# Temporary tiles, gate scaling and quad order around the seven-product stage of a hybrid attention and state-space block

## The chip, the cores and the metric

The kernel runs on one core of one Trainium2 chip. The metric is the device time of one execution in microseconds (us), lower is better. A profile is one execution taken by the hardware profiler; its times are given from the start of its span.

## The reference, cut to what matters

One layer of a hybrid block on 256 tokens of width 2048, all in float32:

```python
hn = rms_norm(x, norm_w)
q, k, v, z_a, z_s, xbc, dt_raw, g_a, g_s = split(hn @ w_in)
o_a = dilated_window_attention(q, k, v, three patterns, mixed) * silu(z_a)
y = ssd_chunked_scan(silu(conv(xbc)), softplus(dt_raw + dt_bias), -exp(a_log)) + d_skip * xs
y = rms_norm(y * silu(z_s), ssm_norm_w)                       # 4096 wide
merged = sigmoid(g_a) * (o_a @ w_attn_branch) + sigmoid(g_s) * (y @ w_ssm_branch)
out = rms_norm(x + merged @ w_out, final_norm_w)
```

The change touches three of these products: `y @ w_ssm_branch` (called ssm in the kernel), and the columns of `hn @ w_in` that give `g_a` (called ga) and `v` (called v).

## The kernel before, in words

Every float32 operand of a matmul is split into a high part h and a low part l, each in a reduced float32 format, and a product is three matmuls: high with high, high with low, low with high. Weights are split on the chip: ScalarE (ACT) copies the loaded weights into h, VectorE (DVE) subtracts h from the weights to give l. Weights arrive by DMA through a ring of tiles named w or wq; h and l have rings of their own (hq and lq for the weights of this stage). From line 702 on each ring has six tiles of 1024 columns (four of the pool stream, two of the pool more).

The stages follow one another on TensorE (PE): first the projections for the state-space part with its scan, then ssm, ga and v, then q, k and the gate of the attention head by head with the attention itself, then the two last products.

The stage of the change works in quads. A quad is a block of 256 rows of the right matrix by 1024 columns, four sub-blocks named 11, 12, 21 and 22, stored by columns as 12, 11 (first half) and 22, 21 (second half). The left factor, 256 tokens wide, is cut into two halves of 128 tokens. A plain quad takes eight block products, 24 matmuls. A seven-product quad (`seven`, after Winograd's form of Strassen's scheme) takes seven, 21 matmuls. It needs sums of sub-blocks on both sides:

- on the right side `quad` (line 623) makes two tiles t13 and t24 of 1024 columns from the loaded weights, with four DVE additions (L647), and splits them as well; both tiles have the tag T with two buffers, in the pool that is passed in;
- on the left side `left` (line 594) makes the sums s1 to s4 of the tokens' blocks, for two quads in one pass of its loop: an addition (L601) that gives the tile x, four more operations (L605 to L608) that give the tile raw, and splits of raw by ACT (L610) and DVE (L611) into sf_y or sf_x and, for s4 of ssm, into yT itself. In the profile x and raw are both called tmp. They come from the same tag T with its two buffers as t13 and t24.

`quads` (line 654) runs one half (cc, 1024 columns) of a product: it goes through the quads in a given order, and behind the last seven-product quad (`u == last`) it adds the accumulators that several results share, into four blocks called sums: ACT copies accumulator 1 (L692), DVE adds (L693 to L696). At the end `finish` combines each sum with an accumulator. For ssm, sums is a tile of the pool mid of its own (tag sums, 2048 columns), and `finish` is `gated`: L731 adds, L732 multiplies into the gate tile th_s. For ga and v the sums lie in the result itself (th_a).

For ssm the order of cc 0 is 0, 2, 4, 1, 6, 8, 3, 10, 12, 5, 11, 9, 13, 7, 14, 15, with seven products in the quads 1, 3, 5, 7 and 9; the left factors for these are made by `left` in three passes (quads 1 and 3, quads 5 and 7, quad 9). After the second quad `then` is called, which is `norm_y` (line 706): eight small matmuls give the sums of squares of y, DVE and GpSimd make the factor (L339, L341, L343, written into the tile small), and two ACT instructions (L716) scale the gate tile th_s, 2048 columns each, with the factor as scale and bias.

After ssm its pool mid is closed and a pool mid2 is opened for ga and v, with T alone in it. `left` is called there for four quads of XT; only the factors of the quads 1, 3 and 5 are used.

The order of the instructions on each engine is set before the run by a planner (`schedule_with_timeline_sim=True`, line 916): it goes by program order as priority, and the splits of the weights in `unit` and `quad` stand 120 places ahead (`L_AHEAD`). Each engine then runs its own list in that order. Within a quad stage the splits of the weights, and the L647 additions, keep their order among themselves (`in_turn`).

Of the kernel before, what the change touches and what calls it, by code (L numbers as in the profile page):

```python
# [9 lines left out]
F32 = mybir.dt.float32  # L10
F32R = mybir.dt.float32r
# [4 lines left out]
P = 128  # L16
# [146 lines left out]
def hybrid_block(ctx: ExitStack, tc: tile.TileContext, wall, wq, xt, x, pk_d, cst_d, fw_d, out):  # L163
# [427 lines left out]
        gates(("gs", 3), th_s, XT)  # L591
        tick(final=True)

    def left(tmp, src, n, h3, l3, h4, l4):
        v = src.rearrange("p (n r) c -> p n r c", r=4)[:, :, 2:4, :]
        for a in range(0, n, 2):
            m = min(2, n - a)
            js = slice(a, a + m)
            x = tmp().rearrange("p (n k s) -> p n k s", n=2, k=2)[:, :m]
            raw = tmp().rearrange("p (n e s) -> p n e s", n=2, e=4)[:, :m]  # L600
            ve.tensor_tensor(x, v[:, js, :, :S].bitcast(F32), v[:, js, :, S:].bitcast(F32), ALU.add)  # L601
            a11, a21 = x[:, :, 0, :P], x[:, :, 0, P:]
            a12, a22 = x[:, :, 1, :P], x[:, :, 1, P:]
            s1, s2, s3, s4 = (raw[:, :, j] for j in range(4))
            ve.tensor_tensor(s1, a22, a21, ALU.subtract)  # L605
            ve.scalar_tensor_tensor(s2, s1, -1.0, a11, ALU.mult, ALU.subtract)
            ve.tensor_tensor(s3, a11, a21, ALU.subtract)
            ve.tensor_tensor(s4, a12, s2, ALU.add)  # L608
            for r, h, l in ((raw[:, :, :3], h3[:, js], l3[:, js]), (s4, h4[:, js], l4[:, js])):
                ac.activation(h, r, AF.Copy)  # L610
                ve.tensor_tensor(l, r, h.bitcast(F32), ALU.subtract)  # L611
# [8 lines left out]
            )  # L620
        behind[key] = ins.ins.name

    def quad(pool, n, seven):
        ws = []
        for j in range(2):
            ws.append(ring("w", f"wq{n}_{j}"))
            nc.sync.dma_start(ws[j], wq[n, :, j * UNIT : (j + 1) * UNIT])
        parts = {}

        def halves(src, names, cut=0):  # L630
            h, l = ring("h", f"hq{n}_{names[1]}"), ring("l", f"lq{n}_{names[1]}")
            in_turn("h", ac.activation(h[:, cut:], src[:, cut:], AF.Copy))  # L632
            in_turn("l", ve.tensor_tensor(l[:, cut:], src[:, cut:], h[:, cut:].bitcast(F32), ALU.subtract))  # L633
            for j, name in enumerate(names):
                parts[name] = h[:, j * 512 : j * 512 + 512], l[:, j * 512 : j * 512 + 512]

        with tc.high_priority(L_AHEAD):
            halves(ws[0], ("12", "11"), 512 if seven else 0)
            halves(ws[1], ("22", "21"))
            if seven:  # L640
                b12, b11, b22, b21 = (w[:, c : c + 512] for w in ws for c in (0, 512))
                t13, t24 = (pool.tile([P, UNIT], F32, name=f"t{n}_{e}", tag="T", bufs=2) for e in range(2))
                for t, a, b in (
                    (t13[:, :512], b12, b11), (t13[:, 512:], b12, b22),
                    (t24[:, :512], t13[:, :512], b22), (t24[:, 512:], t24[:, :512], b21),
                ):
                    in_turn("l", ve.tensor_tensor(t, a, b, ALU.add))  # L647
                halves(t13, (5, 7))
                halves(t24, (6, 4))
        return parts  # L650

    BANKS = {1: "g", 2: "g", 6: "g", 3: "g", 7: "m1", 4: "m1", 5: "m2", 8: "m2"}

    def quads(pool, tag, cc, x_of, n_kt, order, lefts, sums, finish, then=None):
        accs = {}
        last = [u for u in order if u in lefts][-1]

        def product(b, x, w, stop=False):
            first = b not in accs
            if first:  # L660
                accs[b] = bank(BANKS[b], 4 if BANKS[b] == "g" else 2, f"ps_{tag}{cc}_{b}")
            pe.matmul(accs[b], x[0], w[0], start=first, stop=False)  # L662
            pe.matmul(accs[b], x[0], w[1], start=False, stop=False)  # L663
            pe.matmul(accs[b], x[1], w[0], start=False, stop=stop)  # L664

        def block(kt, i):
            x = x_of(kt)
            return x[:, i * P : (i + 1) * P], x[:, S + i * P : S + (i + 1) * P]

        for n, u in enumerate(order):  # L670
            w = quad(pool, QFIRST[tag, cc] + u, u in lefts)
            end = n == len(order) - 1
            k0, k1 = 2 * u, 2 * u + 1
            if u in lefts:
                s1, s2, s3, s4 = lefts[u]
                z = u == last
                product(1, block(k0, 0), w["11"], z)
                product(2, block(k1, 0), w["21"], end)
                product(3, s4, w["22"], end)
                product(7, s3, w[7], z)  # L680
                product(5, s1, w[5], z)
                product(6, s2, w[6], z)
                product(4, block(k1, 1), w[4], end)
            else:
                for b, i, c in ((2, 0, "1"), (3, 0, "2"), (4, 1, "1"), (8, 1, "2")):
                    product(b, block(k0, i), w["1" + c])
                    product(b, block(k1, i), w["2" + c], end)
            if then and n == 1:
                then()
            if u == last:  # L690
                (p1, u4), (u3, u5) = sums
                ac.activation(p1, accs[1], AF.Copy)  # L692
                ve.tensor_tensor(u4, accs[6], p1, ALU.add)  # L693
                ve.tensor_tensor(u3, accs[7], u4, ALU.add)
                ve.tensor_tensor(u4, accs[5], u4, ALU.add)
                ve.tensor_tensor(u5, accs[5], u3, ALU.add)  # L696
        for i, c, b, op in (
            (0, 0, 2, ALU.add), (0, 1, 3, ALU.subtract), (1, 0, 4, ALU.add), (1, 1, 8, ALU.subtract),
        ):
            finish(i, 2 * cc + c, accs[b], sums[i][c], op)  # L700

    more = ctx.enter_context(tc.tile_pool(name="more", bufs=2))
    for tag, dt in (("w", F32), ("h", F32R), ("l", F32R)):
        more.tile([P, UNIT], dt, name=f"first_{tag}", tag=tag, bufs=MORE)
    with tc.tile_pool(name="mid", bufs=2) as mid:
        def norm_y():
            tot = bank("m2", 2, "tot_y")
            for i in range(2):
                for n in range(2):
                    pe.matmul(  # L710
                        tot[:, 2 * i : 2 * i + 2], ssq[:, n, i * P : (i + 1) * P], ones2,
                        start=(n == 0), stop=(n == 1),
                    )
            _, hr = rsqrt_rows(tot[:, 0:4:2], INNER, "y")
            for i in range(2):
                ac.activation(th_s[:, i], th_s[:, i], AF.Identity, scale=hr[:, i : i + 1], bias=hr[:, i : i + 1])  # L716

        sf = mid.tile([P, 5, 2, 3, P], F32R, name="sf_y", tag="sf", bufs=1)
        lefts = {}
        for m, n in enumerate((4, 1)):  # L720
# [1 line left out]
            h3, l3 = s6[:, :, 0], s6[:, :, 1]  # L722
            v = yT[m].rearrange("p (n r) c -> p n r c", r=4)[:, :n, 2]
            h4, l4 = v[:, :, P:S], v[:, :, S + P :]
            left(lambda: mid.tile([P, 1024], F32, name="tmp", tag="T", bufs=2), yT[m], n, h3, l3, h4, l4)
            for j in range(n):
                lefts[8 * m + 2 * j + 1] = [(h3[:, j, e], l3[:, j, e]) for e in range(3)] + [(h4[:, j], l4[:, j])]

# [2 lines left out]
            ve.tensor_tensor(b, a, b, op)  # L731
            ve.tensor_tensor(g, g, b, ALU.mult)  # L732

        for cc, order in enumerate(
            ((0, 2, 4, 1, 6, 8, 3, 10, 12, 5, 11, 9, 13, 7, 14, 15), (1, 0, 2, 3, 4, 6, 5, 8, 10, 7, 11, 12, 9, 13, 14, 15))
        ):
            sums = mid.tile([P, 2, 2, 512], F32, name=f"sums{cc}", tag="sums", bufs=1)
            sums = [[sums[:, i, c] for c in range(2)] for i in range(2)]
            quads(
                mid, "ssm", cc, lambda kt: yT[kt // 16][:, kt % 16, :], 2 * KT, order, lefts, sums, gated,  # L740
                norm_y if cc == 0 else None,
            )

    yo1 = big.tile([P, 2, 2, D], F32, name="th_a", tag="yo1")
    th_a, vt = yo1[:, 0], yo1[:, 1]
    with tc.tile_pool(name="mid2", bufs=2) as mid:
        sf = big.tile([P, 4, 2, 4, P], F32R, name="sf_x", tag="yo0")
        h4, l4 = sf[:, :, 0], sf[:, :, 1]
        left(
            lambda: mid.tile([P, 1024], F32, name="tmp", tag="T", bufs=2), XT, 4,  # L750
            h4[:, :, :3], l4[:, :, :3], h4[:, :, 3], l4[:, :, 3],
        )
        lefts = {2 * j + 1: [(h4[:, j, e], l4[:, j, e]) for e in range(4)] for j in range(4)}

        def gate(i, c, a, b, op):
            ve.tensor_tensor(b, a, b, op)
# [5 lines left out]
        for tag, dst, finish in (("ga", th_a, gate), ("v", vt, value)):  # L762
            for cc in range(2):
                order = (0, 1, 2, 3, 4, 5, 6, 7) if cc or tag == "v" else (0, 2, 4, 1, 6, 3, 5, 7)
                some = {u: lefts[u] for u in (1, 3, 5)}
                sums = [[dst[:, i, (2 * cc + c) * 512 : (2 * cc + c + 1) * 512] for c in range(2)] for i in range(2)]
                quads(mid, tag, cc, lambda kt: XT[:, kt, :], KT, order, some, sums, finish)

    with tc.tile_pool(name="att", bufs=2) as ap, tc.tile_pool(name="ev2", bufs=2) as ev, tc.tile_pool(name="odd2", bufs=2) as odd:
        masks = ap.tile([P, 768], F32, name="masks", tag="masks", bufs=1)  # L770
# [149 lines left out]
```

## Time and profile before

| | |
|---|---|
| median of 3 runs | 1414.25 us (1414.15 to 1415.11) |
| the profiled execution, its own time | 1415.89 us |
| its span, first to last instruction | 1414.1 us |
| mean granted TensorE clock | 0.995 |
| PE busy | 1393.3 us (99%) |
| DVE busy | 1053.8 us (75%) |
| ACT busy | 791.7 us (56%) |
| ssm on PE | 587.61 to 766.43 us |
| ga on PE | 766.43 to 851.36 us |
| v on PE | 851.36 to 934.32 us |

How to read the profile: busy time counts instructions that are in work, for PE with modelled ends; PEld is the loading of weights into TensorE. PEclk is the clock that TensorE was granted, 1.00 or 9 tenths and more at full speed. In a timeline a row gives start, duration, engine, line, operation, output and inputs; `x3` means that three instructions that follow one another are merged, and square brackets give the idle time before the row and what ended it.

### The profile page before, as it was taken

Reading aid. Unit: us, or ns where it says so; the run is one execution under the profiler, and the core shown is the slowest. Engines: PE = TensorE matmul, PEld = TensorE weight load, DVE = VectorE, ACT = ScalarE, POOL = GpSimd, SP = SyncE. Lnnn points to the kernel's source line nnn. Section 1 sums busy time; section 2 is a strip of 40 time slices with the busy share of each in tenths; the row PEclk is TensorE's granted clock in tenths of the full one; section 3 lists DMA queues with packets and bytes.
Section 4 is the critical chain, followed back from the end, with each engine's and each line's share of the span. In section 5 each row is a group of like instructions: output and inputs, shape, how many; then the busy total and the mean of one; then the engine's idle time right before and its main releaser. Section 6 shows DMA issues by size and latency. Waiting matters only on the chain.

```text
span 1414.1 us, 19876 instructions
## 1 busy us (share of the span) xinstructions
PE 1393.3 (99%) x7338; PEld 1183.8 (84%) x7338; DVE 1053.8 (75%) x1551; ACT 791.7 (56%) x1222; POOL 10.1 (1%) x64
## 2 busy tenths in 40 slices
PE   9999999999999999989999999999999999999997
PEld 7788888888888888868888788888888888888886
DVE  5978888877788888778978998876666666655653
ACT  6657766747575757455444566445544545444441
POOL 0000000000000000000000000000000000000000
PEclk9999999999999999989999999999999999999999
DMA  8567656566656666556665575675555555576652
GB/s 330 181 197 229 202 177 210 169 208 203 186 170 211 196 190 183 166 162 205 211 212 190 181 229 182 210 238 179 174 170 176 169 175 171 173 268 186 187 179 74
DMA packets 78049, 272.39 MB, mean 193 GB/s; under 512 B 8768, under 2 KB 9344, under 8 KB 77312
## 3 DMA queue, kind: packets, MB, share of 16 engines
q1 hardware_dynamic: 77376, 270.08, 61.1%
q8 instruction: 57, 0.93, 0.3%
q10 hardware_dynamic: 576, 1.05, 0.2%
q14 instruction: 40, 0.33, 0.1%
HBM read 268.93 MB, written 2.16 MB: 192 GB/s over the span
## 4 chain that ended last, share of the span: by engine, by line
PE 94%; DVE 3%; ACT 1%; issue 1%; DMA 1%; SPq 0%; POOL 0%; POOLq 0%; DVEq 0%; ACTq 0%
PE ps_xs L261 8%; PE ps_zs L261 8%; PE ps_xs L264 4%; PE ps_q L261 4%; PE ps_k L261 4%; PE ps_za L261 4%; PE ps_zs L264 4%; PE ps_ssm L662 4%; PE ps_ssm L663 4%; PE ps_ssm L664 4%; PE ps_k L264 2%; PE ps_za L264 2%; PE ps_q L264 2%; PE ps_attn L329 2%; PE ps_attn L328 2%; PE ps_attn L327 2%
## 5 line engine op out<-in xcount | busy, mean ns | idle before, releaser
L224 DVE TENSOR_TENSOR l<-w,h 128x1024 fp32r<-128x1024 f32 (+1 forms) x353 | 426.6, 1212 | 235.4 <-ACT h L223 232.9
L223 ACT ACTIVATE h<-w 128x1024 fp32r<-128x1024 f32 (+1 forms) x353 | 368.9, 1049 | 373.8 <-PE ps_za L261 50.7
L261 PE MATMUL ps_xs<-XT,h 128*128 128x512 f32 x496 | 174.9, 394 | 0.0
L261 PE MATMUL ps_zs<-XT,h 128*128 128x512 f32 x496 | 174.4, 394 | 0.0
L633 DVE TENSOR_TENSOR lq<-wq,hq 128x1024 fp32r<-128x1024 f32 (+1 forms) x128 | 138.2, 1129 | 39.1 <-ACT hq L632 39.1
L632 ACT ACTIVATE hq<-wq 128x1024 fp32r<-128x1024 f32 (+1 forms) x128 | 119.1, 979 | 67.4 <-PE ps_ssm L664 27.1
L264 PE MATMUL ps_xs<-XT,l 128*128 128x256 f32 x496 | 139.4, 281 | 0.0
L264 PE MATMUL ps_zs<-XT,l 128*128 128x256 f32 x496 | 138.8, 280 | 0.0
L261 PEld LDWEIGHTS ps_zs<-XT,h 128*128 128x128 f32 x496 | 92.9, 187 | 21.4
L261 PEld LDWEIGHTS ps_xs<-XT,h 128*128 128x128 f32 x496 | 93.0, 187 | 21.1
L264 PEld LDWEIGHTS ps_xs<-XT,l 128*128 128x128 f32 x496 | 93.6, 189 | 0.1
L264 PEld LDWEIGHTS ps_zs<-XT,l 128*128 128x128 f32 x496 | 93.6, 189 | 0.0
L261 PE MATMUL ps_q<-XT,h 128*128 128x512 f32 x256 | 90.4, 392 | 0.0
L261 PE MATMUL ps_za<-XT,h 128*128 128x512 f32 x256 | 89.7, 392 | 0.0
L261 PE MATMUL ps_k<-XT,h 128*128 128x512 f32 x256 | 89.7, 392 | 0.0
L632 ACT ACTIVATE hq<-t 128x1024 fp32r<-128x1024 f32 x44 | 46.1, 1060 | 74.0 <-DVE t L647 47.7
L663 PE MATMUL ps_ssm<-lq,yT 128*128 128x512 f32 x216 | 84.3, 390 | 0.0
L664 PE MATMUL ps_ssm<-hq,yT 128*128 128x512 f32 x216 | 84.1, 390 | 0.0
L662 PE MATMUL ps_ssm<-hq,yT 128*128 128x512 f32 x216 | 79.0, 395 | 0.0
L264 PE MATMUL ps_q<-XT,l 128*128 128x256 f32 x256 | 74.5, 291 | 0.0
L264 PE MATMUL ps_k<-XT,l 128*128 128x256 f32 x256 | 71.7, 280 | 0.0
L264 PE MATMUL ps_za<-XT,l 128*128 128x256 f32 x256 | 71.7, 280 | 0.0
(290 smaller groups left out, 2875.6 us busy)
## 6 DMA issues: line engine op xcount, KB each, us to landing
w<-in_wall SPq DMA_DIRECT2D x352, 512.0 KB, 3.7
wq<-in_wq SPq DMA_DIRECT2D x128, 512.0 KB, 4.6
acb<-acum_d SPq DMA_DIRECT2D x32, 256.0 KB, 3.3
th_s<-in_x SPq DMA_DIRECT2D x1, 2048.0 KB, 10.3
fin<-in_x SPq DMA_DIRECT2D x1, 2048.0 KB, 9.2
early<-in_xt SPq DMA_DIRECT2D x7, 256.0 KB, 7.2
fw<-in_fw SPq DMA_DIRECT2D x1, 1024.0 KB, 11.3
out<-fin SPq DMA_DIRECT2D x4, 256.0 KB, 3.0
```

The lines of the kernel that those rows point to most:

```text
L223: ac.activation(h[:, a:b], w[:, a:b], AF.Copy)
L224: ve.tensor_tensor(l[:, a:b], w[:, a:b], h[:, a:b].bitcast(F32), ALU.subtract)
L261: pe.matmul(acc[:width], h[:, kk, :], m, start=(kt == 0), stop=False)
L264: pe.matmul(acc[:width, S:], l[:, kk, :], m[:, :S], start=False, stop=(kt == n_kt - 1))
L327: pe.matmul(accs[i], xh, h, start=(kt == 0), stop=False)
L328: pe.matmul(accs[i], xh, l, start=False, stop=False)
L329: pe.matmul(accs[i], xl, h, start=False, stop=(kt == n_kt - 1))
L632: in_turn("h", ac.activation(h[:, cut:], src[:, cut:], AF.Copy))
L633: in_turn("l", ve.tensor_tensor(l[:, cut:], src[:, cut:], h[:, cut:].bitcast(F32), ALU.subtract))
L662: pe.matmul(accs[b], x[0], w[0], start=first, stop=False)
L663: pe.matmul(accs[b], x[0], w[1], start=False, stop=False)
L664: pe.matmul(accs[b], x[1], w[0], start=False, stop=stop)
```

## The change

- `left` takes its two temporary tiles from the tags s0 and s1 (one buffer of 1024 columns each) by the new function `two`, no longer from T. The sums of ssm now use the same two tags, and are allocated when the last seven-product quad has been issued (`sums` is now a function that is called at that place).
- `norm_y` no longer scales the gate. `scale_gs` scales a piece of 1024 columns of one token half; four pieces are issued, after the quads at places 9 and 11 of cc 0 and after those at places 2 and 4 of cc 1 (places count from 0).
- The order of ssm cc 0 becomes 0, 2, 4, 6, 1, 8, 3, 10, 5, 12, 7, 11, 9, 13, 14, 15: the first seven-product quad stands at place 4, it was at 3, the last at 12, it was at 13 (quad 9, it was quad 7), and between them every second quad has seven products.
- The pool mid stays open from ssm to v; mid2 is gone.
- `left` is called for three quads of XT, it was four; sf_x has three parts.

```diff
-    def left(tmp, src, n, h3, l3, h4, l4):
-        v = src.rearrange("p (n r) c -> p n r c", r=4)[:, :, 2:4, :]
+    def left(src, n, h3, l3, h4, l4):
+        v = src.rearrange("p (n r) c -> p n r c", r=4)[:, :n, 2:4, :]
...
-            x = tmp().rearrange("p (n k s) -> p n k s", n=2, k=2)[:, :m]
-            raw = tmp().rearrange("p (n e s) -> p n e s", n=2, e=4)[:, :m]
+            x, raw = two("left")
+            x = x.rearrange("p (n k s) -> p n k s", n=2, k=2)[:, :m]
+            raw = raw.rearrange("p (n e s) -> p n e s", n=2, e=4)[:, :m]
...
-                t13, t24 = (pool.tile([P, UNIT], F32, name=f"t{n}_{e}", tag="T", bufs=2) for e in range(2))
+                t13, t24 = (mid.tile([P, UNIT], F32, name=f"t{n}_{e}", tag="T", bufs=2) for e in range(2))
...
-            if then and n == 1:
-                then()
+            if n in then:
+                then[n]()
             if u == last:
+                sums = sums()
...
+        def two(name):
+            return [mid.tile([P, UNIT], F32, name=f"{name}_{e}", tag=f"s{e}", bufs=1) for e in range(2)]
...
-            _, hr = rsqrt_rows(tot[:, 0:4:2], INNER, "y")
-            for i in range(2):
-                ac.activation(th_s[:, i], th_s[:, i], AF.Identity, scale=hr[:, i : i + 1], bias=hr[:, i : i + 1])
+            rsqrt_rows(tot[:, 0:4:2], INNER, "y")
+
+        def scale_gs(cc, i):
+            g, r = th_s[:, i, cc * 1024 : (cc + 1) * 1024], hrs[:, 1, i : i + 1]
+            ac.activation(g, g, AF.Identity, scale=r, bias=r)
...
-        for cc, order in enumerate(
-            ((0, 2, 4, 1, 6, 8, 3, 10, 12, 5, 11, 9, 13, 7, 14, 15), (1, 0, 2, 3, 4, 6, 5, 8, 10, 7, 11, 12, 9, 13, 14, 15))
+        def ssm_sums(cc):
+            return [[t[:, c * 512 : (c + 1) * 512] for c in range(2)] for t in two(f"sums{cc}")]
+
+        for cc, order, then in (
+            (0, (0, 2, 4, 6, 1, 8, 3, 10, 5, 12, 7, 11, 9, 13, 14, 15), {1: norm_y, 9: (0, 0), 11: (0, 1)}),
+            (1, (1, 0, 2, 3, 4, 6, 5, 8, 10, 7, 11, 12, 9, 13, 14, 15), {2: (1, 0), 4: (1, 1)}),
         ):
-            sums = mid.tile([P, 2, 2, 512], F32, name=f"sums{cc}", tag="sums", bufs=1)
-            sums = [[sums[:, i, c] for c in range(2)] for i in range(2)]
...
-    with tc.tile_pool(name="mid2", bufs=2) as mid:
-        sf = big.tile([P, 4, 2, 4, P], F32R, name="sf_x", tag="yo0")
+        sf = big.tile([P, 3, 2, 4, P], F32R, name="sf_x", tag="yo0")
...
+        left(XT, 3, h4[:, :, :3], l4[:, :, :3], h4[:, :, 3], l4[:, :, 3])
+        lefts = {2 * j + 1: [(h4[:, j, e], l4[:, j, e]) for e in range(4)] for j in range(3)}
```

More of the change, by code (lines that the diff above doesn't have):

```diff
@@ L621, in in_turn, with quad @@
         behind[key] = ins.ins.name
-    def quad(pool, n, seven):
+    def quad(n, seven):
         ws = []
@@ L652, in hybrid_block, with quads @@
     BANKS = {1: "g", 2: "g", 6: "g", 3: "g", 7: "m1", 4: "m1", 5: "m2", 8: "m2"}
-    def quads(pool, tag, cc, x_of, n_kt, order, lefts, sums, finish, then=None):
+    def quads(tag, cc, x_of, n_kt, order, lefts, sums, finish, then={}):
         accs = {}
@@ L670, in quads @@
         for n, u in enumerate(order):
-            w = quad(pool, QFIRST[tag, cc] + u, u in lefts)
+            w = quad(QFIRST[tag, cc] + u, u in lefts)
             end = n == len(order) - 1
@@ L724, in hybrid_block @@
             h4, l4 = v[:, :, P:S], v[:, :, S + P :]
-            left(lambda: mid.tile([P, 1024], F32, name="tmp", tag="T", bufs=2), yT[m], n, h3, l3, h4, l4)
+            left(yT[m], n, h3, l3, h4, l4)
             for j in range(n):
@@ L732, in gated @@
             ve.tensor_tensor(g, g, b, ALU.mult)
-        for cc, order in enumerate(
-            ((0, 2, 4, 1, 6, 8, 3, 10, 12, 5, 11, 9, 13, 7, 14, 15), (1, 0, 2, 3, 4, 6, 5, 8, 10, 7, 11, 12, 9, 13, 14, 15))
-        ):
-            sums = mid.tile([P, 2, 2, 512], F32, name=f"sums{cc}", tag="sums", bufs=1)
-            sums = [[sums[:, i, c] for c in range(2)] for i in range(2)]
+        def ssm_sums(cc):
[3 more added lines that the diff above has]
+            (1, (1, 0, 2, 3, 4, 6, 5, 8, 10, 7, 11, 12, 9, 13, 14, 15), {2: (1, 0), 4: (1, 1)}),
+        ):
+            then = {n: f if callable(f) else lambda f=f: scale_gs(*f) for n, f in then.items()}
             quads(
-                mid, "ssm", cc, lambda kt: yT[kt // 16][:, kt % 16, :], 2 * KT, order, lefts, sums, gated,
-                norm_y if cc == 0 else None,
-            )
-    yo1 = big.tile([P, 2, 2, D], F32, name="th_a", tag="yo1")
-    th_a, vt = yo1[:, 0], yo1[:, 1]
-    with tc.tile_pool(name="mid2", bufs=2) as mid:
-        sf = big.tile([P, 4, 2, 4, P], F32R, name="sf_x", tag="yo0")
+                "ssm", cc, lambda kt: yT[kt // 16][:, kt % 16, :], 2 * KT, order, lefts, lambda: ssm_sums(cc), gated, then
+            )
+        yo1 = big.tile([P, 2, 2, D], F32, name="th_a", tag="yo1")
+        th_a, vt = yo1[:, 0], yo1[:, 1]
+        sf = big.tile([P, 3, 2, 4, P], F32R, name="sf_x", tag="yo0")
         h4, l4 = sf[:, :, 0], sf[:, :, 1]
[L749 to L753, printed above, removed]
+        left(XT, 3, h4[:, :, :3], l4[:, :, :3], h4[:, :, 3], l4[:, :, 3])
+        lefts = {2 * j + 1: [(h4[:, j, e], l4[:, j, e]) for e in range(4)] for j in range(3)}
         def gate(i, c, a, b, op):
@@ L764, in hybrid_block @@
                 order = (0, 1, 2, 3, 4, 5, 6, 7) if cc or tag == "v" else (0, 2, 4, 1, 6, 3, 5, 7)
-                some = {u: lefts[u] for u in (1, 3, 5)}
                 sums = [[dst[:, i, (2 * cc + c) * 512 : (2 * cc + c + 1) * 512] for c in range(2)] for i in range(2)]
-                quads(mid, tag, cc, lambda kt: XT[:, kt, :], KT, order, some, sums, finish)
+                quads(tag, cc, lambda kt: XT[:, kt, :], KT, order, lefts, lambda: sums, finish)
     with tc.tile_pool(name="att", bufs=2) as ap, tc.tile_pool(name="ev2", bufs=2) as ev, tc.tile_pool(name="odd2", bufs=2) as odd:
```

## The prediction

> **What bounds the kernel now.** The page comes first.
>
> ```profile
> span 1414.1 us, 19876 instructions
> ...
> PE 1393.3 (99%) x7338; PEld 1183.8 (84%) x7338; DVE 1053.8 (75%) x1551; ACT 791.7 (56%) x1222; POOL 10.1 (1%) x64
> ...
> PEld 7788888888888888868888788888888888888886
> ...
> PEclk9999999999999999989999999999999999999999
> ```
>
> TensorE sets the time, and only what stops or slows it counts. Its busy share, 99%, shows little of a stop; two rows of slices (40, of 35.35 us each) do. In slice 17, counted from 0, which is 601.0 to 636.3 us, the weight loads fall from 8 tenths to 6 and the granted clock from 9 to 8, and in slice 22, from 777.8 us, the weight loads fall to 7. Apart from the first two slices and the last nothing else falls under 8. The list of what PE waited for, over the whole span, has five lines, and only these two lie in the stages that the change touches:
>
> ```profile
> PE ps_ssm L662 <- ACT hq L632: 6.8, 2, 5.9
> PE ps_ga L662 <- ACT hq L632: 1.1, 3, 0.7
> ```
>
> PE waits 6.8 us in ssm and 1.1 us in ga for an ACT copy of weights. What each costs in all comes from the timeline, whose rows have start, duration, engine and line, and from the windows (length; busy PE, PEld, DVE, ACT, POOL; granted clock; DMA share; GB/s):
>
> ```profile
> 587.61 0.50 PE L662 MATMUL ps_ssm<-hq,yT 128*128 128x512 f32 x1
> 598.63 0.95 PE L710 MATMUL tot_y<-small,ssq 128*128 128x2 f32 x8
> 599.43 1.42 PE L662 MATMUL ps_ssm<-hq,yT 128*128 128x512 f32 x5
> 606.83 0.39 PE L664 MATMUL ps_ssm<-hq,yT 128*128 128x512 f32 x1
> 613.17 1.19 PE L662 MATMUL ps_ssm<-hq,sf_y 128*128 128x512 f32 x2 [5.95 <-ACT hq L632]
> 615.20 0.79 PE L662 MATMUL ps_ssm<-hq,sf_y 128*128 128x512 f32 x1 [0.84 <-ACT hq L632]
> 766.43 0.39 PE L662 MATMUL ps_ga<-hq,XT 128*128 128x512 f32 x1
> 851.36 0.39 PE L662 MATMUL ps_v<-hq,XT 128*128 128x512 f32 x1
> 934.32 0.39 PE L261 MATMUL ps_q<-XT,h 128*128 128x512 f32 x1
> ```
>
> ```profile
> 610.00:611.00 1.00, 0.00 (x0) 0.00 (x0) 0.93 (x4) 0.72 (x2) 0.00 (x0) 0.82 0.00 0
> 620.00:621.00 1.00, 1.00 (x4) 0.75 (x3) 1.00 (x2) 0.00 (x0) 0.00 (x0) 0.56 0.99 344
> ```
>
> By the code a half of ga or v is 5 plain quads of 24 matmuls and 3 of 21, 183 in all, and a half of ssm is 11 x 24 + 5 x 21 = 369. v, without a wait, takes 934.32 - 851.36 = 82.96 us for 366, so 0.2267 us each. ssm takes 766.43 - 587.61 = 178.82 us; its 738 matmuls are worth 167.28, the tot_y matmuls 599.43 - 598.63 = 0.80, and **10.74 us are lost**. ga takes 84.93 for what v does in 82.96: **1.97 us lost**. The ssm loss is the two waits, 6.8 us, and half speed behind them. The clock falls at about 610.6 (0.82 in that microsecond, half of it from then on) and is back at 620.88 (0.56); matmuls run from 613.17, so (620.88 - 613.17 - 0.84) / 2 = 3.4 us go there. That is 10.2 of 10.74.
>
> Why ACT was late:
>
> ```profile
> 598.24 2.52 ACT L632 ACTIVATE hq<-wq 128x1024 fp32r<-128x1024 f32 x3
> 603.35 4.09 ACT L716 ACTIVATE th_s<-th_s,small 128x2048 f32<-128x2048 f32 x2 [2.60 <-DVE small L343]
> 607.34 0.82 ACT L610 ACTIVATE sf_y<-tmp 128x768 fp32r<-128x768 f32 x1
> ...
> 611.97 1.06 ACT L632 ACTIVATE hq<-t 128x1024 fp32r<-128x1024 f32 x1 [0.99 <-DVE t L647]
> ```
>
> ```profile
> 604.13 0.69 DVE L601 TENSOR_TENSOR tmp<-yT 128x512 f32<-128x512 f32 x1
> 608.19 0.96 DVE L611 TENSOR_TENSOR sf_y<-tmp,sf_y 128x768 fp32r<-128x768 f32 x1 [3.37 <-ACT sf_y L610]
> ...
> 610.58 0.69 DVE L647 TENSOR_TENSOR t<-wq 128x512 f32<-128x512 f32 x1
> 611.19 0.68 DVE L647 TENSOR_TENSOR t<-wq,wq 128x512 f32<-128x512 f32 x1
> ```
>
> ACT runs its list in order. The gate scaling occupies it from 603.35 for 4.09 us, the split of the second pass of left (L610) follows, DVE stands idle 3.37 us until it is through, and t13, which needs a tile T that left holds, starts at 610.58. Its ACT copy is what PE gets at 613.17.
>
> **The change part by part.** Durations from the groups of 586 to 690 and 586 to 770 us (busy, mean ns, idle before) and from the tile tmp (minimum/median/maximum ns):
>
> ```profile
> L632 ACT ACTIVATE hq<-wq 128x1024 fp32r<-128x1024 f32 x30 | 30.4, 1053 | 16.8 <-PE ps_ssm L664 12.3 <-issue 3.4 <-DMA wq<-in_wq 0.6
> L716 ACT ACTIVATE th_s<-th_s,small 128x2048 f32<-128x2048 f32 x2 | 4.1, 2092 | 2.6 <-DVE small L343 2.6
> ```
>
> ```profile
> L633 DVE TENSOR_TENSOR lq<-wq,hq 128x1024 fp32r<-128x1024 f32 x57 | 67.4, 1221 | 26.5 <-ACT hq L632 26.4
> L647 DVE TENSOR_TENSOR t<-t,wq 128x512 f32<-128x512 f32 x20 | 13.8, 690 | 0.3
> L633 DVE TENSOR_TENSOR lq<-wq,hq 128x512 fp32r<-128x512 f32 x10 | 6.9, 686 | 0.0
> ```
>
> ```profile
> L605 DVE TENSOR_TENSOR tmp<-tmp x5: 292/422/426, 594.3 to 777.9; 128x256 f32<-128x256 f32 x4, 128x128 f32<-128x128 f32 x1
> L601 DVE TENSOR_TENSOR tmp<-yT x3: 691/1224/1226, 593.1 to 604.1; 128x1024 f32<-128x1024 f32 x2, 128x512 f32<-128x512 f32 x1
> L611 DVE TENSOR_TENSOR sf_y<-tmp,sf_y x3: 553/950/957, 597.1 to 611.8; 128x768 fp32r<-128x768 f32 x2, 128x384 fp32r<-128x384 f32 x1
> ```
>
> *Gate pieces.* 2 x 2.09 us leave ACT at 603; four pieces come later. A piece of 1024 columns isn't in the trace; it lies between the copy of that width, 1.05, and a little over half of 2.09, say 1.14. All four wait for nothing by then, and behind each in ACT's list stands a weight copy that can come up to 1.14 us later. ACT is idle before its 30 wide copies for 16.8 us in 586 to 690, so I price this at 0, at most 1.14. The Trainium skill (ScalarE: Activation LUTs, What ACT_TABLE_LOAD costs) has a fixed part of about 280 ns in every activation with a pointer as bias, by which four pieces take 4.53 us and the two old ones 3.97: it speaks against cutting, by 0.56 us of ACT's time. The measured 2.09 is 0.1 above its 1.99. By that rule the sum is the same as long as ACT has the idle time named above.
>
> *Left's tiles, one plain quad more.* t13 no longer waits for tmp, and PE gets there later by 24 x 0.2267 = 5.44 us. The last matmul before the stop started at 606.83; the next would have come at 607.06, so PE now asks for the copy of t13 at 612.50 and for its low part at 612.73. Now DVE, from the row at 604.13. By then it must in addition have split the new plain quad (one split of 1.22 where a 0.69 stood: 0.53) and the halves of the first seven-product quad (0.69 + 1.22): 2.44, so 606.57. From there: L601 0.69; L611 of the second pass 0.95 + about 0.42 (256 columns, as L605); t13 2 x 0.69; that makes 610.0. The third pass, 4 x 0.29, stands ahead of t13 in program order: 611.2. The copy on ACT, 1.06, ends at 611.1 to 612.2, in time for 612.50. Behind it t24 2 x 0.69, L611 of the third pass 0.55 + about 0.29, low part of t13 1.22: 612.6 without the third pass, 614.6 with it. Rows follow one another sooner than they last (611.19 - 610.58 = 0.61 for 0.69), so some 14 of them give back about 1.1: 611.5 to 613.5, and a piece of the gate ahead of L610 could add 1.1 to that. Against 612.73 the wait that stays is 0 to 1.9 us; I take 1.2, nearer to the upper end since the third pass stands ahead. A wait of that size costs no clock: the clock above fell 3.5 us after PE had stopped, and the waits in ga, 0.7 at the longest, left no mark on it. **Gain 10.74 - 1.2 = 9.5 us.** Quads 1 and 6 change places in SP's list of loads as well, same size and number; DMA moved nothing at 610 to 611 since the rings were full, so 0.
>
> *Seven products in every second quad of cc 0.* v has this order already; two turns of DVE there:
>
> ```profile
> 857.46 4.10 DVE L633 TENSOR_TENSOR lq<-wq,hq 128x1024 fp32r<-128x1024 f32 x4 [1.18 <-ACT hq L632]
> ...
> 867.66 4.10 DVE L633 TENSOR_TENSOR lq<-wq,hq 128x1024 fp32r<-128x1024 f32 x4 [1.14 <-ACT hq L632]
> ```
>
> A turn is 10.20 us, PE's (24 + 21) x 0.2267, and DVE has 1.1 us of it left. 0, and DVE catches up on a late start at 1.1 us a turn.
>
> *One pool, three quads on the left of XT.* Left of XT needs s0 and s1, whose last readers (L732) are DVE's own, ahead of it in the same list: no wait. One pass is half as wide: L601 0.53, four of L605's kind 0.52, L611 0.40, so DVE has 1.45 us less. Whether the ga loss of 1.97 goes with it hangs on these rows:
>
> ```profile
> 799.04 0.60 ACT L692 ACTIVATE th_a<-ps_ga 128x512 f32<-128x512 f32 x1 [4.01 <-PE ps_ga L664]
> 799.54 2.00 ACT L632 ACTIVATE hq<-t 128x1024 fp32r<-128x1024 f32 x2
> ```
>
> ```profile
> 797.68 1.41 DVE L647 TENSOR_TENSOR t<-t,wq 128x512 f32<-128x512 f32 x2
> ```
>
> t13 was ready at 797.68, but in ACT's list its copy stands behind L692, which stood 4.01 us waiting for a PE product until 799.04. An earlier t13 alone changes nothing; only another order of these two would. I count 0. The pool open through v costs 0: no wait of PE stands at q or v, and the tags s0, s1 and sf are long out of use when the attention's tiles come.
>
> Sum against the profiled execution, 1415.89 us (span 1414.1 and 1.8 around it): 1406.4. It lies 1.64 above the median of 1414.25; the loss is in the program and not in that difference, so the forecast for the median is 1414.25 - 9.5 = **1404.7 us**.
>
> **The rivals.** *The planner also turns the pair in ga* (t13's copy ahead of L692). For: DVE's t13 comes 1.45 us earlier in its plan. Against: the order in the program is untouched. 1404.7 - 1.97 = 1402.7, and 1401.5 if the first wait vanishes too.
>
> *The change doesn't do what it says:* all four pieces are ready as soon as small is written, at 603.3, ACT waits there anyway (2.60 us), and the planner pulls them forward. Then 4 x 1.05 to 1.14 stand where 4.09 stood, the copies of the first seven-product quad (0.62 + 1.05) follow at about 607.7 to 609.4, its last low part ends at 610.6, t13 at 612, its copy at 613, its low part at 614.5 to 616: a wait of 2 to 3.3 us, so 1405.5 to 1406.8. Against: L610 and weight copies come first by priority wherever they are ready. Past 3.5 us of stop the clock falls as well, another 3.4: up to 1410.5. The Trainium skill (TensorE: Matmul & The Clock Gate, Part 1) puts that point at one idle window of about 3.4 us, free-running; the trace agrees with 3.5, and the rule would let a stop of that length go either way.
>
> *DVE becomes the bound (slower).* If a turn of a plain and a seven-product quad took DVE in cc 0 of ssm over 10.20 + 3.5 us, each of its four turns would stop PE by 3.5 and halve the clock for 3.4 more: 4 x 6.9 = 27.6, so 1414.25 - 10.74 + 27.6 = 1431. It decides from 3.4 us a turn, (10.74 + 2.8) / 4. Against: the turns of v, at 9.1.
>
> **How the numbers follow.** A measurement of this kernel can tell about 0.2%, 2.8 us, from no change. Forecast 0.47 (1403.5 without a wait, 1406.5 with 1.9 of wait and 1.1 for a gate piece); ga turned too 0.27; pieces pulled forward 0.16; the first stop stays nearly whole, for a cause not seen here, 0.06, of which 0.04 is within 0.2%; slower 0.04. The range takes the first two whole and the pulled-forward case without the clock's fall, with a little for a second wait: 1401.5 to 1408. Faster 0.92, same 0.04, slower 0.04.
>
> **What would show it.** Right: no row 4 us long on ACT near 603; four rows of 1024 columns on th_s, near 650 to 665 and 690 to 715; the first seven-product matmuls on sf_y at about 612 to 614 with a wait under 2 us; a granted clock of 1.00 from 605 to 625; first matmul of ga 9.5 us earlier; t written while left of yT still runs. Wrong: pieces at 603 to 608, a clock below 1.00 near 615, a new line in PE's waits at places 6 to 12 of cc 0, or a ga stage other than 84.9 us.

## The result and the profile after

The changed kernel takes 1403.05 us (median of 4 runs, 1402.63 to 1403.84); the kernel before, beside it, 1414.53 us (4 runs, 1414.15 to 1415.11). The ratio is 0.9917, 95% interval 0.9905 to 0.993: faster by 11.5 us. The profiled execution took 1403.24 us, 12.65 less than that of before.

The page of the changed kernel, its rows for span, engines, weight loads by slice and granted clock by slice:

```profile
span 1401.5 us, 19875 instructions
...
PE 1388.3 (99%) x7338; PEld 1181.6 (84%) x7338; DVE 1051.2 (75%) x1551; ACT 791.6 (56%) x1224; POOL 10.6 (1%) x64
...
PEld 7788888888888888888888888888888888888886
...
PEclk9999999999999999999999999999999999999999
```

The dips in slices 17 and 22 are gone. The list of what PE waited for has three lines now, all of them far from the changed stages:

```profile
PE ps_gs L328 <- DVE l L224: 2.0, 3, 1.2
PE warm L368 <- POOL raw_C L461: 1.4, 1, 1.4
PE ps_first L285 <- ACT h L223: 1.2, 2, 0.7
```

The first matmuls of ssm, ga, v and q on the timeline of the changed kernel, where the lines from 601 to 705 have moved down by one or two and the gate, L716 before, is L723:

```profile
587.38 0.50 PE L663 MATMUL ps_ssm<-hq,yT 128*128 128x512 f32 x1
...
755.74 0.39 PE L663 MATMUL ps_ga<-hq,XT 128*128 128x512 f32 x1
...
838.70 0.39 PE L663 MATMUL ps_v<-hq,XT 128*128 128x512 f32 x1
...
921.66 0.39 PE L261 MATMUL ps_q<-XT,h 128*128 128x512 f32 x1
```

By the arithmetic of the prediction (738 matmuls of 0.2267 us and 0.80 for tot_y in ssm, 82.96 in ga) ssm now loses 168.36 - 168.08 = 0.28 us, it was 10.74, and ga 0.00, it was 1.97. The two give 12.43 of the 12.65 us. The rest, about 0.2, lies ahead of ssm, which starts at 587.38 and started at 587.61; behind ga nothing changed.

How it came about differs from what the diff says. Gate, copies and additions on ACT and DVE of the changed kernel:

```profile
597.94 4.41 ACT L633 ACTIVATE hq<-wq 128x1024 fp32r<-128x1024 f32 x5
604.18 4.65 ACT L723 ACTIVATE th_s<-th_s,small 128x1024 f32<-128x1024 f32 x4 [1.83 <-DVE small L343]
608.74 1.04 ACT L633 ACTIVATE hq<-t 128x1024 fp32r<-128x1024 f32 x1
...
610.72 1.04 ACT L633 ACTIVATE hq<-t 128x1024 fp32r<-128x1024 f32 x1
```

```profile
605.19 0.69 DVE L648 TENSOR_TENSOR t<-wq 128x512 f32<-128x512 f32 x1
605.79 0.69 DVE L648 TENSOR_TENSOR t<-wq,wq 128x512 f32<-128x512 f32 x1
606.39 0.42 DVE L607 SCALAR_TENSOR_TENSOR left<-left,left 128x256 f32<-128x256 f32 x1
```

```profile
612.26 0.62 PE L663 MATMUL ps_ssm<-hq,sf_y 128*128 128x512 f32 x2
```

The "late" gate pieces run at 604.18, all four, 4.65 us long, where 4.09 us of gate stood before. What is new is that t13 is made at 605.19, in the middle of left's second pass, since it needs no tile of left's any more; its copy follows the gate at once and is done at 609.78, and PE asks for it at 612.26.

### The profile page after: what moved, and what is told of

It reads as the page before. It is cut to its first block, busy times and chain, and to the rows that moved or that the text cites. A ratio compares the mean times of both kernels' runs of the same rounds, so it can differ in the third digit from the quotient of the medians.

```text
span 1401.5 us, 19875 instructions
## 1 busy us (share of the span) xinstructions
PE 1388.3 (99%) x7338; PEld 1181.6 (84%) x7338; DVE 1051.2 (75%) x1551; ACT 791.6 (56%) x1224; POOL 10.6 (1%) x64
## 3 DMA queue, kind: packets, MB, share of 16 engines
q10 hardware_dynamic: 576, 1.05, 0.2%
## 4 chain that ended last, share of the span: by engine, by line
PE 97%; DVE 2%; ACT 0%; DMA 0%; issue 0%; SPq 0%; POOL 0%; POOLq 0%; DVEq 0%; ACTq 0%
PE ps_xs L261 8%; PE ps_zs L261 8%; PE ps_xs L264 4%; PE ps_q L261 4%; PE ps_k L261 4%; PE ps_za L261 4%; PE ps_zs L264 4%; PE ps_ssm L663 4%; PE ps_ssm L664 4%; PE ps_ssm L665 4%; PE ps_k L264 2%; PE ps_za L264 2%; PE ps_q L264 2%; PE ps_attn L329 2%; PE ps_attn L327 2%; PE ps_attn L328 2%
```

## The experiments

**Theories.** *Tiles and order:* the ssm loss hangs on t13 and t24 being late for PE; t13 gets early by its own tiles, and PE comes 5.44 us later by the order; the gate's cut does nothing, since the planner puts the pieces where the whole was. *Gate:* cutting and issuing it late is what pays. *Order alone:* one more plain quad is enough. For ga: DVE's 1.45 us, or the pool and tiles.

Both kernels and the twelve experiments in one table: first matmuls of ssm, ga and v on the timeline, the losses worked out as above, the stretch ahead of the last matmul in which the clock was halved, worked out from one-microsecond windows (below), and the median of the timed runs (one run where marked 1). The kernel before was run again beside the experiments, with medians from 1415.06 to 1415.52; a difference of a few tenths between rows of the last column says nothing, and the losses are the finer measure.

| | ssm | ga | v | ssm loss | ga loss | half clock | us |
|---|---|---|---|---|---|---|---|
| before | 587.61 | 766.43 | 851.36 | 10.74 | 1.97 | 10.24 | 1414.53 |
| changed | 587.38 | 755.74 | 838.70 | 0.28 | 0.00 | none | 1403.05 |
| e1 changed, gate whole | 587.94 | 756.31 | 839.27 | 0.29 | 0.00 | none | 1403.31 |
| e2 before, four gate pieces | 587.92 | 766.55 | 851.48 | 10.55 | 1.97 | 10.24 | 1416.00 |
| e3 before, tiles | 587.50 | 761.38 | 846.32 | 5.80 | 1.98 | 3.42 | 1410.84 |
| e4 before, order | 587.93 | 761.25 | 846.19 | 5.24 | 1.98 | 3.40 | 1411.10 |
| e5 changed, gate held late | 587.87 | 756.23 | 839.19 | 0.28 | 0.00 | none | 1403.71 |
| e6 changed, old order, gate held late | 587.31 | 757.35 | 840.31 | 1.96 | 0.00 | none | 1404.94 |
| e7 changed, shared T | 587.18 | 761.28 | 844.24 | 6.02 | 0.00 | 3.40 | 1408.74 (1) |
| e8 changed, four quads of XT | 587.61 | 756.07 | 839.87 | 0.38 | 0.84 | none | 1404.40 (1) |
| e9 before, gate held late | 587.04 | 762.16 | 847.12 | 7.04 | 2.00 | 6.84 | 1411.61 |
| e10 before, three quads of XT | 587.78 | 765.76 | 849.56 | 9.90 | 0.84 | 6.82 | 1414.06 (1) |
| e11 changed, old order | 587.22 | 761.19 | 844.15 | 5.89 | 0.00 | 3.40 | 1408.68 (1) |
| e12 before, tiles and order | 587.64 | 756.01 | 840.93 | 0.29 | 1.96 | none | 1405.36 |

**e1, the changed kernel with the gate whole.**

```diff
-            rsqrt_rows(tot[:, 0:4:2], INNER, "y")
+            _, hr = rsqrt_rows(tot[:, 0:4:2], INNER, "y")
+            for i in range(2):
+                ac.activation(th_s[:, i], th_s[:, i], AF.Identity, scale=hr[:, i : i + 1], bias=hr[:, i : i + 1])
...
-            (0, (0, 2, 4, 6, 1, 8, 3, 10, 5, 12, 7, 11, 9, 13, 14, 15), {1: norm_y, 9: (0, 0), 11: (0, 1)}),
-            (1, (1, 0, 2, 3, 4, 6, 5, 8, 10, 7, 11, 12, 9, 13, 14, 15), {2: (1, 0), 4: (1, 1)}),
+            (0, (0, 2, 4, 6, 1, 8, 3, 10, 5, 12, 7, 11, 9, 13, 14, 15), {1: norm_y}),
+            (1, (1, 0, 2, 3, 4, 6, 5, 8, 10, 7, 11, 12, 9, 13, 14, 15), {}),
```

> The changed kernel with the gate scaled whole, by two activations of 2048 columns behind the second quad, as before. Tiles theory (the loss in ssm hangs on t13 waiting for the tiles of left, and is gone once t13 has tiles of its own and PE comes one plain quad later; the four pieces stand in the same ACT gap as the two old instructions did): about 1403.0 us, loss in ssm 0.3 us. Gate theory (the cut and delay of the scaling is what pays): the ssm loss comes back in good part, 1408 us or more.

Measured: 1403.31 us, ratio to before 0.9914 (0.9899 to 0.9929), ssm loss 0.29. The gate theory falls: without its cut the whole gain is there.

**e2, before with four gate pieces.** `scale_gs` as in the change, and:

```diff
-                norm_y if cc == 0 else None,
+                {1: norm_y, 9: lambda: scale_gs(0, 0), 11: lambda: scale_gs(0, 1)} if cc == 0
+                else {2: lambda: scale_gs(1, 0), 4: lambda: scale_gs(1, 1)},
```

> The kernel before with only the gate cut into four pieces that are issued at the late places. Tiles theory: the planner pulls the four pieces forward to about 603 us, 4.65 us of ACT where 4.09 stood, so nothing is gained: about 1414.5 to 1415.5 us, loss in ssm about 10.7 to 11.5 us, four pieces in one row on ACT before 610 us. Gate theory: 1408 us or less.

Measured: 1416.00 us, ratio 1.0003 (0.9993 to 1.0012). The gate on ACT, and PE's wait:

```profile
603.55 4.64 ACT L718 ACTIVATE th_s<-th_s,small 128x1024 f32<-128x1024 f32 x4 [2.60 <-DVE small L343]
```

```profile
PE ps_ssm L662 <- ACT hq L632: 7.2, 2, 6.4
```

As expected, but for a time 0.5 us above the expected span: the planner pulls the pieces forward, and the edit by itself is worth nothing.

**e3, before with the tiles.**

```diff
-            x = tmp().rearrange("p (n k s) -> p n k s", n=2, k=2)[:, :m]
-            raw = tmp().rearrange("p (n e s) -> p n e s", n=2, e=4)[:, :m]
+            x, raw = (t() for t in tmp)
...
-            left(lambda: mid.tile([P, 1024], F32, name="tmp", tag="T", bufs=2), yT[m], n, h3, l3, h4, l4)
+            left([lambda e=e: mid.tile([P, 1024], F32, name=f"tmp{e}", tag=f"s{e}", bufs=1) for e in range(2)], yT[m], n, h3, l3, h4, l4)
...
+            def sums(cc=cc):
+                ts = [mid.tile([P, 1024], F32, name=f"sums{cc}_{e}", tag=f"s{e}", bufs=1) for e in range(2)]
```

> The kernel before with only the temporary tiles of left for ssm taken from s0 and s1, shared with the sums; T is left to t13 and t24. Tiles theory: t13's copy comes before the gate scaling, but PE asks for it at 607 and t24's copy stands behind 4.09 us of gate: a wait of about 3 us at about 608, loss in ssm 3 to 6 us, 1407 to 1410 us. Order theory (the one more plain quad is what pays): no gain, 1414 us.

Measured: 1410.84 us, ratio 0.9968 (0.9956 to 0.9979), ssm loss 5.80, inside the expected 3 to 6; the time lies 0.84 us above the expected span. ACT, and the matmul behind the long stop:

```profile
604.48 1.06 ACT L633 ACTIVATE hq<-t 128x1024 fp32r<-128x1024 f32 x1 [3.79 <-DVE small L343]
605.45 4.07 ACT L718 ACTIVATE th_s<-th_s,small 128x2048 f32<-128x2048 f32 x2
...
610.46 1.04 ACT L633 ACTIVATE hq<-t 128x1024 fp32r<-128x1024 f32 x1
```

```profile
611.56 0.50 PE L663 MATMUL ps_ssm<-hq,sf_y 128*128 128x512 f32 x1 [2.83 <-ACT hq L633]
```

t13's copy stands ahead of the gate now, at 604.48, and is in time. The copy of t24 stands behind it at 610.46, and PE waits for that one, 2.83 us. In the changed kernel t24's copy is at 610.72, no earlier; there PE comes later.

**e4, before with the order.**

```diff
-            ((0, 2, 4, 1, 6, 8, 3, 10, 12, 5, 11, 9, 13, 7, 14, 15), (1, 0, 2, 3, 4, 6, 5, 8, 10, 7, 11, 12, 9, 13, 14, 15))
+            ((0, 2, 4, 6, 1, 8, 3, 10, 5, 12, 7, 11, 9, 13, 14, 15), (1, 0, 2, 3, 4, 6, 5, 8, 10, 7, 11, 12, 9, 13, 14, 15))
```

> The kernel before with only the order of the quads in the first half of ssm changed, first seven-product quad at place 4. t13 still waits for left's tiles behind the gate, its copy ends at about 614 to 614.5, and PE asks at 612.5. Tiles theory: waits of 2 to 3 us stay and the clock holds, loss in ssm 2 to 4 us, 1406 to 1408 us. Order theory: the loss is gone, 1403 to 1405 us.

Measured: 1411.10 us, ratio 0.997 (0.9958 to 0.9981), ssm loss 5.24 where 2 to 4 was expected. Order alone is not enough; t13 still waits for left's third pass (DVE), its copy is late (ACT), and PE stops twice:

```profile
611.72 0.29 DVE L608 TENSOR_TENSOR tmp<-tmp 128x128 f32<-128x128 f32 x1
612.05 0.69 DVE L647 TENSOR_TENSOR t<-wq 128x512 f32<-128x512 f32 x1
```

```profile
613.45 1.06 ACT L632 ACTIVATE hq<-t 128x1024 fp32r<-128x1024 f32 x1 [1.01 <-DVE t L647]
```

```profile
614.65 0.70 PE L662 MATMUL ps_ssm<-hq,sf_y 128*128 128x512 f32 x2 [1.67 <-ACT hq L632]
616.68 0.80 PE L662 MATMUL ps_ssm<-hq,sf_y 128*128 128x512 f32 x1 [1.33 <-ACT hq L632]
```

The waits are as expected, 3.0 us together. What the expectation had wrong is the clock: it was to hold, and was halved for 3.4 us. Two windows of e4 (the granted clock is third from the end):

```profile
616.00:617.00 1.00, 0.32 (x1) 0.32 (x2) 0.93 (x2) 1.00 (x2) 0.00 (x0) 0.64 0.53 172
619.00:620.00 1.00, 1.00 (x4) 0.84 (x3) 1.00 (x2) 0.99 (x2) 0.00 (x0) 0.66 0.10 41
```

A window that starts at full clock and ends at half has a mean of 1 - 0.5 x share at half: 0.64 puts the fall at 616.28, 0.66 the return at 619.68, 3.40 us.

**e12, before with tiles and order,** the edits of e3 and e4 together, run last.

> The kernel before with two edits and no other: the tiles of left for ssm from s0 and s1, and the new order of the quads in the first half. Gate whole and early, two pools, four quads on the left of XT as before. Tiles and order theory: loss in ssm 0.3 us, all 10.5 of it gained, ga still loses 1.97 us: about 1405.2 us. If the two alone are not enough (each left 5 to 6 us): loss in ssm 3 us or more, 1408 us.

Measured: 1405.36 us, ratio 0.993 (0.9913 to 0.9946); ssm loss 0.29, ga loss 1.96. These two edits are the whole of the ssm gain, with the gate whole and early:

```profile
604.48 4.09 ACT L718 ACTIVATE th_s<-th_s,small 128x2048 f32<-128x2048 f32 x2 [1.83 <-DVE small L343]
608.47 1.04 ACT L633 ACTIVATE hq<-t 128x1024 fp32r<-128x1024 f32 x1
```

**e5, the changed kernel with the gate held late, and e6, the same with the old order.** The piece is put into the chain that keeps the weight copies in turn:

```diff
-            ac.activation(g, g, AF.Identity, scale=r, bias=r)
+            in_turn("h", ac.activation(g, g, AF.Identity, scale=r, bias=r))
```

> The changed kernel with the four gate pieces held in the list of the weight copies, so that the planner cannot pull them forward: each stands behind the copies of the quad after which it is issued. If the pieces at 604 us cost nothing in the changed kernel: 1403.0 to 1403.5 us, loss in ssm 0.3 us, no row of the gate on ACT near 604. If the change still pays for them there: 0.3 us or more faster.

> The changed kernel with the order of the quads before (first seven-product quad at place 3), and the gate pieces held late in the same way. Tiles and gate theory (with tiles of its own t13 is early, and without the gate on ACT the copy of t24 is too, so the later quad is not needed): waits under 1 us, loss in ssm 0.3 to 1.5 us, about 1403 to 1404.5 us. Order theory (without one more plain quad something stays): loss in ssm 3 us or more, 1406 us.

e5 measured 1403.71 us (1403.51 to 1404.06), 0.2 above the expected span, ssm loss 0.28. The pieces do run late there, the tile th_s on ACT:

```profile
L723 ACT ACTIVATE th_s<-th_s,small x4: 1231/1233/1235, 632.7 to 689.7; 128x1024 f32<-128x1024 f32 x4
```

So the changed kernel pays nothing for its early pieces, and holding them late gains nothing. e6 measured 1404.94 us (ratio 0.9929, 0.9912 to 0.9945), ssm loss 1.96 where 0.3 to 1.5 was expected by the one theory and 3 or more by the other: between the two. PE's only wait in its ssm is for DVE, not ACT:

```profile
PE ps_ssm L664 <- DVE lq L634: 1.0, 2, 0.6
```

With tiles of its own and no gate in front of t24, the earlier quad costs 1.96 - 0.28 = 1.7 us, of which the list names 1.0 as waits. So tiles and a late gate take most of the ssm loss without the new order, but not all of it.

**e7, the changed kernel with left's tiles back in T.**

```diff
-            x, raw = two("left")
+            x, raw = (mid.tile([P, UNIT], F32, name=f"left_{e}", tag="T", bufs=2) for e in range(2))
```

> The changed kernel with left's temporary tiles back in T, for ssm and for XT; order, late-issued pieces, one pool and three quads stay. Tiles theory: as with the order alone, first stop at about 613 to 614 and another behind it, half a clock for one stretch, loss in ssm 5 to 6.5 us, about 1408.5 to 1409.5 us with ga at 82.96 us. If the tiles do not matter once the order is there: loss 0.3 us.

Measured, one run: 1408.74 us, ssm loss 6.02, ga 0.00. As expected, e4's picture with a gate 0.55 us longer.

**e11, the changed kernel with the old order.**

```diff
-            (0, (0, 2, 4, 6, 1, 8, 3, 10, 5, 12, 7, 11, 9, 13, 14, 15), {1: norm_y, 9: (0, 0), 11: (0, 1)}),
+            (0, (0, 2, 4, 1, 6, 8, 3, 10, 12, 5, 11, 9, 13, 7, 14, 15), {1: norm_y, 9: (0, 0), 11: (0, 1)}),
```

> The changed kernel with the order of the quads before; the four gate pieces issued late and so free to be pulled forward. As with the tiles alone, with 0.55 us more of gate on ACT ahead of the copy of t24: a stop of about 3.4 us at 608.5, the clock at half speed behind it for 3.4 us, loss in ssm 6 to 7 us; ga without loss; about 1409 us.

Measured, one run: 1408.68 us, ssm loss 5.89, a hair under the expected 6 to 7: one wait of 3.4 us, and half clock for 3.40 us. e7 and e11 say from the changed kernel's side what e4 and e3 say from the other: each of tiles and order alone leaves about half of the loss, 5.2 to 6.0 of 10.74 us.

**e9, before with the gate held late,** the edits of e2 and, in its `scale_gs`, the `in_turn` of e5.

> The kernel before with the gate in four pieces that are held late in the list of the weight copies; tiles and order as before. What a gate that really comes late does by itself: L610 of the second pass runs at 604, but t13 still waits for the tiles of left, its copy comes at about 608.5 and ends at 609.6, PE asks at 607.1: waits of 2.5 and 0.8 us. Loss in ssm 3.5 us if the clock holds, 5 to 5.5 us if a stretch of 3.4 us at half speed follows; 1407.5 to 1409.5 us.

Measured: 1411.61 us, ratio 0.9976 (0.9965 to 0.9986), ssm loss 7.04, above both figures expected. Copy of t13 and the two stops:

```profile
607.79 1.06 ACT L632 ACTIVATE hq<-t 128x1024 fp32r<-128x1024 f32 x1 [0.99 <-DVE t L647]
```

```profile
608.99 0.70 PE L662 MATMUL ps_ssm<-hq,sf_y 128*128 128x512 f32 x2 [2.34 <-ACT hq L632]
611.02 0.79 PE L662 MATMUL ps_ssm<-hq,sf_y 128*128 128x512 f32 x1 [1.32 <-ACT hq L632]
```

The wait is 3.7 us, it was 6.8; the clock takes its part for twice 3.4 us, not once:

```profile
609.00:610.00 1.00, 0.69 (x2) 0.26 (x2) 0.97 (x3) 0.09 (x1) 0.00 (x0) 0.79 0.73 225
616.00:617.00 1.00, 1.00 (x5) 0.81 (x4) 1.00 (x2) 0.21 (x1) 0.00 (x0) 0.79 0.82 270
```

So the gate was a part of the old loss, 10.74 - 7.04 = 3.7 us of it, but a part that disappears of itself once tiles and order are there.

**e8, the changed kernel with four quads of XT, and e10, before with three.**

```diff
-        sf = big.tile([P, 3, 2, 4, P], F32R, name="sf_x", tag="yo0")
+        sf = big.tile([P, 4, 2, 4, P], F32R, name="sf_x", tag="yo0")
...
-        left(XT, 3, h4[:, :, :3], l4[:, :, :3], h4[:, :, 3], l4[:, :, 3])
+        left(XT, 4, h4[:, :, :3], l4[:, :, :3], h4[:, :, 3], l4[:, :, 3])
```

e10 is the same edit the other way, in `left` and its call of the kernel before.

> The changed kernel with left of XT made for four quads again. If the ga loss of 1.97 us went by the 1.45 us that DVE saves there: ga loses 1 to 2 us again. If it went by the tiles and the one pool: ga stays at 82.96 us, a loss under 0.3. ssm as in the changed kernel, loss 0.3 us.

> The kernel before with left of XT made for three quads, T and the pools as before. ssm as before, loss 10 to 11 us. ga: if DVE's 1.45 us is all that was wanted, no loss; if the pool and tiles have a part, 0.5 to 1.2 us of loss stay of the 1.97.

Both measured a ga loss of 0.84, between 1.97 and 0. For e8 that is neither of the two cases expected, for e10 it is the one in which pool and tiles have a part. Three quads alone (e10) take 1.13 us of it, the rest of the change without them (e8) takes 1.13 as well, and only both together take all. ACT around L694 (accumulator 1 copied) in e8, and the same place in the changed kernel:

```profile
786.72 1.07 ACT L633 ACTIVATE hq<-t 128x1024 fp32r<-128x1024 f32 x1 [2.59 <-DVE t L648]
788.69 0.60 ACT L694 ACTIVATE th_a<-ps_ga 128x512 f32<-128x512 f32 x1 [0.90 <-PE ps_ga L665]
789.18 1.05 ACT L633 ACTIVATE hq<-t 128x1024 fp32r<-128x1024 f32 x1
```

```profile
786.15 1.06 ACT L633 ACTIVATE hq<-t 128x1024 fp32r<-128x1024 f32 x1 [2.58 <-DVE t L648]
787.48 1.06 ACT L633 ACTIVATE hq<-t 128x1024 fp32r<-128x1024 f32 x1 [0.27 <-PE ps_ga L665]
...
791.29 0.57 ACT L694 ACTIVATE th_a<-ps_ga 128x512 f32<-128x512 f32 x1
```

Before, L692 stood ahead of both copies of t. In e8 and e10 it stands between them, in the changed kernel behind both. The order goes with how early DVE makes t24 for this place: its additions begin 31.25 us after the first matmul of ga in the kernel before and in e12, 30.45 and 30.43 in e8 and e10, and 30.21 in the changed kernel. That the planner turns the pair because of this is argued from these four figures, not tried.

What the rest of the change adds to the three quads can be narrowed down. e1 loses nothing with the gate whole, e6 nothing with the old order, and e7 nothing with left's tiles in T, so none of these is needed; e12 has the tiles of ssm and the order and loses all of it. That leaves the one pool. In the trace of e8 and of the changed kernel left of XT begins 2.78 us after the first matmul of ga, ahead of the last multiplication into th_s; in the kernel before, e10 and e12, with two pools, it begins 4.52 us after, behind it. The pool was not tried by itself.

## Why the prediction was right, and where its steps were not

The range, 1401.5 to 1408, held the time, and the sign and the place were right: of the two losses that it had measured out, 10.46 of the 10.74 us and all of the 1.97 went. Of the cases it was not the forecast (1404.7) that came true but the better one, "the planner also turns the pair in ga", at its lower figure: 1401.5 by the sum, 1403.05 measured. Most of the 1.55 us between comes from one step, "the loss is in the program and not in that difference": the profiled execution of before lay 1.36 above the median of its runs (1415.89 against 1414.53), that of the changed kernel 0.19, so the profiles gained 12.65 us and the medians 11.48. That the time lies only 1.65 us below the forecast is in part luck: two terms of the sum were too high, the wait that stays by 1.2 us and ga by 1.97, and these 1.2 us stand against them.

- *What bounds the kernel:* right. The two waits, the half clock behind the first, the PE counts. "Why ACT was late" named the gate first and T second. The runs put it otherwise: with tiles and order the gate may stand there (e1, e12), without them its removal gives 3.7 us (e9).
- *Gate pieces,* "come later", priced at 0 and at 1.05 to 1.14 us each: 0 was right, for another reason. They did not come later; "pulled forward" was a rival with 0.16, and its mechanism is what happened. Its price, 2 to 3.3 us, did not come, because the step that put the copies of the first seven-product quad behind the pieces failed: they stood ahead of the gate (among the five copies from 597.94). A piece took 1.23 us (e5: 1.231 to 1.235), above both bounds. The prediction counted one pointer, the bias; the gate has two, scale and bias. The Trainium skill (ScalarE: Activation LUTs, What ACT_TABLE_LOAD costs) adds about 93 ns for each pointer operand, by which an estimate gives 1.23 us for 1024 columns and 2.08 for 2048; the traces agree, with 1.23 and 2.09.
- *The wait that stays,* 1.2 us: mis-sized, it was nothing. The sum had t13 made behind L601 and L611, and perhaps behind left's third pass too, by 610.0 to 611.2. In the run its additions began at 605.19 and ended at 606.48: with T free, the planner put them ahead of L607 of the second pass. The sum had taken DVE's order from the old list, in which T enforced it.
- *A wait of that size costs no clock:* its reason failed, and without harm only because no stop stayed. The prediction took it that the clock falls only about 3.5 us after PE has stopped; behind stops of 1.67 and 1.33 us in e4, and one of 2.83 in e3, it was halved. A single stop of 1.2 us was not measured.
- *Every second quad with seven products:* right. DVE's splits of a turn begin at 623.75, 632.73 and 641.71 in the changed kernel, 8.98 apart against PE's 10.20, so DVE catches up by 1.2 us a turn; the prediction said 1.1.

```profile
623.75 4.09 DVE L634 TENSOR_TENSOR lq<-wq,hq 128x1024 fp32r<-128x1024 f32 x4
...
632.73 4.09 DVE L634 TENSOR_TENSOR lq<-wq,hq 128x1024 fp32r<-128x1024 f32 x4
...
641.71 4.09 DVE L634 TENSOR_TENSOR lq<-wq,hq 128x1024 fp32r<-128x1024 f32 x4
```

- *ga,* counted 0: wrong by its 1.97. "An earlier t13 alone changes nothing; only another order of these two would" was the right question, and 0.27 for that order too little: with three quads, and so less DVE work ahead of that place, it moved over half the way in e10 (1.13 of 1.97 us), and all the way with the rest of the change.

## What to carry to other kernels

Where a planner orders the engines' lists, where an instruction is issued in the program says little about when it runs: to have it late, tie it to something late (e5); to have something early, free the tile it waits for (e3), and read the new list before pricing. A stop that is a chain of several late things is not divided among its causes: here a late gate alone took away 3.7 us, the tiles alone 4.9, the order alone 5.5, tiles and order together 10.45, and then nothing was left for the gate. When a stop is priced, the half clock behind it counts too: in the kernel before 3.4 us on top of 6.8.

## What the runs showed of the hardware that was not expected

The lengths say that the clock went down and up on a raster, a grid of equal steps in time. The half-clock stretches were 3.40 (e4, e7, e11), 3.42 (e3), 6.82 (e10), 6.84 (e9) and 10.24 us (before, e2): one, two or three times 3.41 us, each costing half its length where PE had work. Length of the stop alone doesn't decide. e3's windows are the closest case:

```profile
612.00:613.00 1.00, 0.78 (x4) 0.45 (x3) 1.00 (x3) 1.00 (x2) 0.00 (x0) 1.00 0.00 0
613.00:614.00 1.00, 1.00 (x5) 0.76 (x4) 1.00 (x2) 1.00 (x2) 0.00 (x0) 0.71 0.00 0
...
616.00:617.00 1.00, 1.00 (x4) 0.76 (x4) 1.00 (x3) 1.00 (x2) 0.00 (x0) 0.58 0.88 299
```

The fall is at 613.42 (0.71), 1.86 us after the long stop had ended at 611.56. The 3.41 us ahead of the fall hold 0.78 + 0.42 us of work and 0.44 from 611 to 612, 1.64 or 48%; the stretch ahead of that one, with the first part of the stop in it, holds about 62% and the clock held. It held in e10 behind one of 53% (605.56 to 608.97). The return came behind a stretch of that length with PE busy for 88% or more (e4: 0.32 of the first 0.72 us, then all), and not behind one of about 75% (before, 614.05 to 617.47). The Trainium skill (TensorE: Matmul & The Clock Gate, Part 1) has the window of about 3.4 us and that it runs free; the lengths agree. The same part of the Trainium skill gives as the rule that PE must have no idle gaps of more than about 3.4 us; here shorter ones were enough, 2.83 us in e3 and 3.0 in two parts in e4.

e10 has the same two stops in ssm as before (5.97 and 0.84 us against 5.95 and 0.84). Yet its stretch was 6.82 where before had 10.24, and its loss 9.90 where before had 10.74: the place of a stop on the raster, it seems, changed its price by 0.84 us. The runs of before, 1413.65 to 1417.59 over all comparisons, scatter wider than the four of the changed kernel, 1402.63 to 1403.84, which fits this; the raster of a single run is not on record.
